# A hybrid attention encoder on one core: values turned on VectorE in 32 by 32 blocks instead of on TensorE, and stored in 128-byte pieces

## The chip, the cores and the metric

The kernel runs on one core of a Trainium2 chip. A core has five engines with instruction streams of their own: PE (TensorE, the matrix engine, which also turns tiles by a matmul with the identity), DVE (VectorE), ACT (ScalarE), POOL (GpSimd) and SP (SyncE, which here issues nearly all DMAs, in one queue). On-chip memory is SBUF, 128 partitions wide; matmuls write to PSUM banks, of which there are eight; everything else lies in DRAM. The metric is the device time of one execution in microseconds (us), lower is better. Before the change it is 1909.06 us (median of 3 runs, 1908.71 to 1910.85).

## The reference, cut to what matters

One encoder layer is applied to two groups of tokens (2048 and 512) with shared weights. A combined projection makes ten pieces; branch A is neighbourhood attention on a grid 64 tokens wide, branch B windowed attention with two key/value heads.

```python
u = rms_norm(h, norm_g)
proj = u @ w_in
qa, ka, va, za, qb, kb, vb, zb, ga, gb = jnp.split(proj, cuts, axis=-1)
o_a = neighbourhood_attention(qa, ka, va, na_rpb, n)      # softmax(q k^T / 8 + bias) @ v
o_b = window_attention(qb, kb, vb, t5_bias, sink, n)
y_a = (o_a * jax.nn.silu(za)) @ w_proj_a
y_b = (o_b * jax.nn.silu(zb)) @ w_proj_b
merged = jax.nn.sigmoid(ga) * y_a + jax.nn.sigmoid(gb) * y_b
return h + merged @ w_out                                 # then a final rms_norm
```

All values are 32-bit floats. The projection leaves features on the partitions and tokens along the free axis. The product of probabilities and values needs the values the other way, with tokens (keys) on the partitions: somewhere `va` and `vb` have to be turned. That turning is what the change is about.

## The kernel before

**Precision by splitting.** Each operand x of a matmul is held as a high part h (x cast to the matmul's reduced type) and a low part l = x - h, and a product is made of three matmuls, h·h, h·l and l·h. So each tensor that is written for a later matmul is written twice, h beside l.

**Windows and features.** The 2560 tokens are handled as five windows (here also called token blocks) of 512 tokens (`WTOK`), numbered 0 to 4. The projection's outputs are 42 features of 128 columns: QA is 0 to 3, KA 4 to 7, VA 8 to 11, ZA 12 to 15, QB 16 to 19, KB 20, VB 21, ZB 22 to 25, then the gates. A VA feature holds two heads of 64 columns.

**Stages.** (1) `beside` projects features of window 4 while the operands for windows 0 and 1 are prepared. (2) A pass over all 42 features in 21 pairs, with the windows 0 and 1 (`pairs`, called by `pass_`). (3) `beside` again, and a second pass with windows 2 and 3. (4) Attention of all windows, with the dense layers mixed in. (5) The end of window 4. Stages 2 and 3 are the passes of this document; by the trace the first runs from about 130 us, the second from about 650 us, and the attention begins near 985 us.

**A pair in a pass.** Two features by two windows are a 2 by 2 block product, done with Strassen's seven products (`product`, line 762) in place of eight. Each product is 12 matmuls of 128x128 by 128x512. Sums of weights for it are made on POOL (`sides`, lines 728 to 741) and split by ACT and DVE (`split_part`, lines 189 and 190); weights are fetched two pairs ahead (`wraw`, `raw`). The product results lie in five PSUM banks (`pa`, `pc`, `pe`, ...). Four of them per pair become finished features: `store` adds what is missing, and hands the result on by kind. The order of the pairs is the list `order`, taken two by two: QA, QA, KA, KA, VA, VA, QB, QB, KB with VB, ZA, ...

**A value feature before.** `store` adds into a tile `tkv`; for VA `columns` (line 263 is its work in `combine`) writes it with the tokens permuted, so that 128 neighbouring columns are 16 grid columns by 8 rows. Two products later (`later(lag[0], ...)`, counted off by `tick`, which `product` calls) `put_v` turns it: `transposed` (line 606) does four 128x128 matmuls against the identity into a PSUM bank `vt`; ACT copies the high part (line 235) and DVE subtracts for the low part (line 236) into `vn`; SP stores `vn` to DRAM (`va` for branch A, two DMAs; `vb` for branch B, one).

**Tiles that matter.** `vn`, `evq`, `evk` and `eva`, that is all finished features on their way to DRAM, rotate through the four buffers of tag `ev` in the pool `ev`: a fifth has to wait until the store of the first has landed. `tkv` rotates through three buffers of tag `t`.

**What sets the order.** In stages 1 to 3 the orders of PE and of SP are those of the program text (`manual_schedule`), the orders of DVE, ACT and POOL are set by a scheduler that plays a time model. SP issues its DMAs in order and waits at the head for what the next one needs. The DMAs on SP's queue carry eight completion semaphores in turn, and each issue waits for the DMA that had the same semaphore before, that is for the one eight places earlier.

**The readers of the values.** In the attention of branch A `unit_a` loads `va` and picks, for block b of 8 grid columns, the slice `v_block(b)` of its middle axis (line 1037): the store puts the even blocks in places 0 to 3 and the odd ones in places 4 to 7.

Of the kernel before, what the change touches and what calls it, by code (L numbers as in the profile page):

```python
# [10 lines left out]
F32R = mybir.dt.float32r  # L11
# [6 lines left out]
P = 128  # L18
# [33 lines left out]
def a_kind_width(kind):  # L52
# [17 lines left out]


def v_block(b):

    return b % 2 * 4 + b // 2


def b_blocks(w, n):
# [10 lines left out]
def encoder_block(ctx: ExitStack, tc: tile.TileContext, xT, x_end, w_in, w_pa, w_pb, w_o, norm_g, final_g,  # L88
# [41 lines left out]
    def move(out, in_):  # L130
        last_move[0] = nc.sync.dma_start(*(f32(a) if a.dtype == F32R else a for a in (out, in_)))
        return last_move[0]
# [418 lines left out]
    def later(steps, fn, *args):  # L551
        queue.append([steps, fn, args])
# [49 lines left out]
    def transposed(dst, src, nch, n):  # L602
# [5 lines left out]
        dv = dst[:n, :, :nch].rearrange("p g c (h f) -> p c g h f", h=2)  # L608
        split(dv[:, :, :, 0, :], dv[:, :, :, 1, :], tv)

    def put_v(br, w, p, t):
        vn = ev.tile([P, 2, 4, P], F32R, tag="ev", name="vn")
        transposed(vn, t, 4, P)
        if br == "a":

            for x in range(2):
                dst = va_d[p][:, w * 64 : (w + 1) * 64, 4 * x : 4 * x + 4].rearrange("g p k f -> p g k f")
                move(dst, vn[64 * x : 64 * x + 64])
        else:
            move(vb_d[w * WTOK : (w + 1) * WTOK].rearrange("(c p) g f -> p g c f", p=P), vn)  # L620

    def put_v_meta(br, p, src):
        vm = st.tile([N_META, 2, 1, P], F32R, tag="vm", name="vm", bufs=1)
        transposed(vm, src, 1, N_META)
        if br == "a":
            if p == 0:
                zr = ev.tile([P, WTOK], F32, tag="t", name="zr", bufs=3)[:, :P]
                nc.vector.memset(zr, 0.0)
                for d in vrow_d:
                    move(d.rearrange("c b g f -> (c b g) f"), zr)  # L630
            n = len(META_COLS)
            for y in range(2):
                b = v_block(META_COLS[0] // 8 + y)
                move(vrow_d[p][:, b : b + n].rearrange("c b g f -> c b (g f)"),
                     vm[8 * y : 8 * y + 8].rearrange("m g o f -> m o (g f)").broadcast_to([8, n, 2 * P]))
        else:
            move(vbm_d, vm[:, :, 0])

    def columns(f, t, ps, other, c0, n):

        if VA <= f < ZA:
            r0, r1 = c0 // GRID_W, (c0 + n) // GRID_W
            ps, o = (x.rearrange("p (r b c) -> p b r c", b=8, c=8) for x in (ps, ps if other is None else other[1]))
            other = other and (other[0], o)
            dst = t.rearrange("p (b r c) -> p b r c", b=8, c=8)[:, :, r0:r1]
        else:
            dst = t[:, c0 : c0 + n]
        combine(dst, ps, other)

    def put_kv(f, w, src):  # L650
        if f < VA:
            put_k("a", w, f - KA, src)
        elif f < ZA:
            later(lag[0], put_v, "a", w, f - VA, src)
        elif f == KB:
            put_k("b", w, 0, src)
        else:
            later(lag[0], put_v, "b", w, 0, src)

    def store(f, w, ps, other):  # L660

        if f < KA:
            put_q("a", w, f, ps, other)
        elif KA <= f < ZA or f in (KB, VB):
            src = ps
            if other is not None or VA <= f < ZA or f == VB:
                src = ev.tile([P, WTOK], F32, tag="t", name="tkv", bufs=3)
                columns(f, src, ps, other, 0, WTOK)
            put_kv(f, w, src)
        elif f < QB:  # L670
            put_act(z_d["a", w, f - ZA], AF.Silu, ps, other)
        elif f < KB:
            put_q("b", w, f - QB, ps, other)
        elif f < GA:
            put_act(z_d["b", w, f - ZB], AF.Silu, ps, other)
        else:
            put_gate(w, f, ps, other)
# [202 lines left out]
                pass  # L880
        return a, first, raw1

    order = [*range(0, ZA), *range(QB, ZB), *range(ZA, QB), *range(ZB, 42)]
    both = list(zip(order[::2], order[1::2]))
    firsts = [*range(QA, KA), *range(QB, KB), *range(KA, ZA), KB, VB]
    rest = [f for f in range(GA) if f not in firsts]
# [93 lines left out]
    def unit_a(w, p, h, g, sh):  # L980

        grows, i0, k0, kr = a_window(w)
        R = kr + 1
        kind = a_kind(w)
        t0 = (0 if w == 0 else DEC_SEQ) + k0 * GRID_W
        nt = kr * GRID_W
        c0, C = CG[g]
        n = R * C
        nb, kb = C // 8, R * 8
        hs = slice(64 * h, 64 * h + 64)  # L990
        qs = slice(g * P, (g + 1) * P)
        if g == 0 and h == 0:
            q = sh["q"] = ld.tile([P, 2, 2, WTOK], F32R, tag="q", name="q")
            move(q.rearrange("p h i t -> p h (i t)"), qa_d[w, p].rearrange("(h d) j x -> (d j) h x", h=2))
        if g == 0 and h == 1:
            z = sh["z"] = ld.tile([P, WTOK], F32, tag="z", name="z")
            move(z, z_d["a", w, p])
        if g == 0:
            kd = sh["kd"] = ld.tile([P, R, GRID_W], F32R, tag="kd", name="kd")
            move(kd[:, 1:, :].rearrange("p r c -> p (r c)"),  # L1000
                 ka_d[p][hs].rearrange("d i t -> (d i) t")[:, t0 : t0 + nt])
            move(kd[:, 0, :], kam_d[p][hs].rearrange("d i t -> (d i) t"))
            v = sh["v"] = ld.tile([P, 8, P], F32R, tag="v", name="v", bufs=3)
            move(v[8:kb], va_d[p][h, t0 // 8 : t0 // 8 + kb - 8])
            move(v[:8], vrow_d[p][:, :, h])
            b = sh["b"] = ld.tile([P, a_kind_width(2)], F32, tag="ba", name="ba")
            move(b[:, : a_kind_width(kind)], bias_a[kind][2 * p + h])
        q, kd, v, z, bias = (sh.get(x) for x in ("q", "kd", "v", "z", "b"))
        yield
        if g == 0 and h == 0:  # L1010
            sh["y"] = at.tile([P, WTOK], F32, tag="y32", name="y32")
        y32 = sh["y"]
        s = ps_s.tile([P, WTOK], F32, tag="s", name="s")
        sv = s[:, :n].rearrange("p (r c) -> p r c", r=R)
        nc.tensor.matmul(sv, q[:, h, 0, qs], kd[:, :, c0 : c0 + C], start=True, stop=False)
        nc.tensor.matmul(sv, q[:, h, 1, qs], kd[:, :, c0 : c0 + C], start=False, stop=True)
        b0 = R * (0, 24, 24, 56)[g]
        nm = scores_max(s, n, bias[:, b0 : b0 + n])
        pr = at.tile([P, 2 * HALF], F32, tag="pr", name="pr", bufs=3)[:, :WTOK]
        sm = sums_of()[:, :1]  # L1020
        exps(pr[:, :n].rearrange("p (b r c) -> p r b c", b=nb, c=8), sv.rearrange("p r (b c) -> p r b c", c=8), nm, sm)
        yield
        normalise(pr[:, :n], inverse(sm), on_act=g == 1)
        yield
        tp = ps_p.tile([P, WTOK], F32, tag="tp", name="tp")
        for i, b in enumerate(A_ORDER[g]):
            nc.tensor.transpose(tp[:kb, i * P : (i + 1) * P], pr[:, b * kb : (b + 1) * kb], ident)  # L1027
        a = slice(A_FIRST[g], A_FIRST[g] + 2 * nb - 1, 2)
        tb = tp[:kb, : nb * P].rearrange("p (b t) -> p b t", t=P)
        nc.scalar.copy(ph_[:kb, a], tb)  # L1030
        nc.vector.tensor_sub(pl_[:kb, a], tb, f32(ph_[:kb, a]))  # L1031
        yield
        if g == 1:
            sh["o"] = ps_o.tile([P, WTOK], F32, tag="o", name="oa")
        o = sh.get("o")
        for i, (part, b, x, gs) in enumerate(A_PRODUCTS[g]):
            vb = v[:kb, v_block(b), :]
            cols = slice(gs[0] * P, (gs[-1] + 1) * P)
            src = (ph_ if part == "h" else pl_)[:kb, x : x + len(gs)].rearrange("p b t -> p (b t)")

            if part == "h":
                nc.tensor.matmul(o[:, cols], vb, src, start=g == 1 and i == 0, stop=False, skip_group_check=True)  # L1042
            else:
                nc.tensor.matmul(o[:64, cols], vb[:, :64], src, start=False, stop=(g, i) == (3, 5),  # L1044
                                 skip_group_check=True)
        if g == 3:
            ol = at.tile([64, WTOK], F32, tag="ol", name="ol", bufs=1)
            nc.scalar.copy(ol, o[64:128])
            nat = "p (g r c) -> p g r c"
            nc.vector.tensor_add(y32[hs].rearrange("p (r g c) -> p g r c", g=4, c=16),  # L1050
                                 o[:64].rearrange(nat, g=4, c=16), ol.rearrange(nat, g=4, c=16))
            if h == 1:
                nc.gpsimd.tensor_mul(y32, y32, z)
                y_split("a", w, p, y32)
        yield
# [509 lines left out]
```

## Time and profile before

| | |
|---|---|
| runs | 1908.71, 1909.06, 1910.85 us |
| profiled execution, its own time | 1908.84 us |
| its span in the trace | 1906.5 us |
| PE busy | 1878.5 us, 99% |
| DVE / ACT / POOL busy | 69% / 60% / 38% |
| share of the 16 DMA engines' time, SP's queue | 66.8% |

A span is shorter than the time of its execution, here by 2.3 us. A row of a group of instructions gives the engine, the operation, the tiles (written <- read), how many there were, and their duration (least, median, largest, or busy time and mean). A waiting instruction shows in the lists of waits, with the one that ended the wait behind the arrow. PE's records overlap, since a matmul begins while the one before is still draining: starts, not durations, tell how long PE is taken.

### The profile page before, as it was taken

The page shows a single profiled execution, that of the slowest core. Times are in us where ns is not written, and L with a number is a line of the kernel's source. Part 1 is how long each engine was busy: PE and PEld are TensorE (multiplying, and loading weights), DVE is VectorE, ACT ScalarE, POOL GpSimd, SP SyncE. Part 2 cuts the span into 40 slices and gives each one's busy share as a digit, 9 for nine tenths or more (in the row PEclk, how much of TensorE's full clock was granted, in tenths as well). Part 3 has the DMA queues.
Part 4 walks back from the last instruction along what each step waited for, and adds up shares of the span by engine and source line. Part 5 has one row for each costly group of instructions (what it writes and reads, how often), then busy time and mean ns, then how long its engine had stood idle before and what let it go on. Part 6 is the DMA issues. An engine that isn't in the chain of part 4 may idle for free.

```text
span 1906.5 us, 29720 instructions
## 1 busy us (share of the span) xinstructions
PE 1878.5 (99%) x9925; PEld 1599.4 (84%) x9925; DVE 1320.3 (69%) x2887; ACT 1147.6 (60%) x2515; POOL 731.9 (38%) x556
## 2 busy tenths in 40 slices
PE   8999999999999999999999999999999999999998
PEld 6998888888888888888878888888888888888886
DVE  8886455556477544445457788878987887888874
ACT  6454443434464444444356787797788788878932
POOL 2005342323103232323223335655844773585420
PEclk9999999999999999999999999999999999999999
DMA  7667554645296765644368877977986996697473
GB/s 261 218 190 293 175 198 165 218 174 177 83 353 218 239 210 194 194 138 160 105 207 289 254 217 261 294 223 242 319 270 185 307 316 217 197 326 252 124 289 141
DMA packets 223760, 423.78 MB, mean 222 GB/s; under 512 B 49640, under 2 KB 90808, under 8 KB 222072
## 3 DMA queue, kind: packets, MB, share of 16 engines
q1 hardware_dynamic: 223320, 421.88, 66.8%
q8 instruction: 79, 1.29, 0.3%
q14 instruction: 73, 0.60, 0.1%
q10 hardware_dynamic: 288, 0.01, 0.0%
HBM read 303.07 MB, written 118.74 MB: 221 GB/s over the span
## 4 chain that ended last, share of the span: by engine, by line
PE 75%; DVE 9%; ACT 6%; DMA 5%; issue 3%; POOL 2%; SPq 0%; ACTq 0%; DVEq 0%; POOLq 0%
PE pa L762 21%; PE pe L762 10%; PE pc L762 5%; PE mm L135 4%; PE mm L137 4%; PE mm L136 4%; PE tp L1027 2%; PE pso L137 2%; PE pso L135 2%; PE pso L136 2%; PE tp L1129 1%; PE oa L1044 1%; PE oa L1042 1%; DVE s L953 1%; DMA wo<-wos 1%
## 5 line engine op out<-in xcount | busy, mean ns | idle before, releaser
L190 POOL TENSOR_TENSOR wt<-wraw,wt 128x512 fp32r<-128x512 f32 x164 | 215.4, 1331 | 288.2 <-ACT wt L189 288.1
L762 PE MATMUL pa<-u,wt 128*128 128x512 f32 x1008 | 242.9, 390 | 0.0
L762 PE MATMUL pa<-u,x 128*128 128x512 f32 x984 | 237.8, 390 | 0.0
L189 ACT CAST wt<-wraw 128x512 fp32r<-128x512 f32 x312 | 177.9, 620 | 73.8 <-PE mm L137 37.6
L762 PEld LDWEIGHTS pa<-u,wt 128*128 128x128 f32 x1008 | 188.7, 188 | 39.0
L762 PEld LDWEIGHTS pa<-u,x 128*128 128x128 f32 x984 | 183.9, 188 | 38.1
L733 POOL TENSOR_TENSOR s<-wraw,raw 128x512 f32<-128x512 f32 x40 | 57.9, 1447 | 271.7 <-DVE x L190 271.7
L135 PE MATMUL mm<-u,wt 128*128 128x512 f32 (+2 forms) x416 | 151.6, 364 | 7.3 <-ACT u L316 7.3
L728 POOL TENSOR_TENSOR s<-raw 128x512 f32<-128x512 f32 x40 | 60.0, 1500 | 253.3 <-DMA raw<-in_w_in_dram 137.0
L136 PE MATMUL mm<-u,wt 128*128 128x512 f32 (+2 forms) x416 | 147.5, 355 | 1.5 <-DVE u L317 1.5
L137 PE MATMUL mm<-u,wt 128*128 128x512 f32 (+2 forms) x416 | 147.5, 355 | 0.8 <-DVE wt L190 0.8
L190 DVE TENSOR_TENSOR wt<-wraw,wt 128x512 fp32r<-128x512 f32 x148 | 104.6, 746 | 61.6 <-ACT wt L189 61.5
L762 PE MATMUL pe<-u,wt 128*128 128x512 f32 x504 | 121.9, 391 | 0.0
L762 PE MATMUL pc<-u,wt 128*128 128x512 f32 x504 | 121.1, 389 | 0.0
L1031 DVE TENSOR_TENSOR pl<-tp,ph 128x512 fp32r<-128x512 f32 (+7 forms) x160 | 98.8, 617 | 24.0 <-ACT ph L1030 22.3
L762 PE MATMUL pe<-u,x 128*128 128x512 f32 x480 | 115.3, 389 | 0.0
L960 ACT ACTIVATE pr<-s,nm 128x384 f32<-128x384 f32 (+5 forms) x160 | 91.3, 571 | 37.9 <-DVE nm L953 35.4
L762 PEld LDWEIGHTS pc<-u,wt 128*128 128x128 f32 x504 | 94.6, 188 | 19.6
L762 PEld LDWEIGHTS pe<-u,wt 128*128 128x128 f32 x504 | 94.2, 188 | 19.4
L741 POOL TENSOR_TENSOR s<-wraw,s 128x512 f32<-128x512 f32 x40 | 52.9, 1322 | 146.2 <-DVE wt L190 146.2
L1030 ACT CAST ph<-tp 128x512 fp32r<-128x512 f32 (+7 forms) x160 | 84.7, 529 | 38.7 <-PE tp L1027 36.5
L135 PE MATMUL pso<-mh,wt 128*128 128x512 f32 x256 | 107.1, 418 | 0.0
(238 smaller groups left out, 5050.7 us busy)
## 6 DMA issues: line engine op xcount, KB each, us to landing
wraw<-in_w_in_dram SPq DMA_DIRECT2D x86, 512.0 KB
qa<-evq SPq DMA_DIRECT2D x20, 1024.0 KB
raw<-in_w_in_dram SPq DMA_DIRECT2D x40, 512.0 KB
q<-qa SPq DMA_DIRECT2D x20, 1024.0 KB
wraw<-in_w_o_dram SPq DMA_DIRECT2D x32, 512.0 KB
kbt<-kb SPq DMA_DIRECT2D x32, 384.0 KB
qb<-evq SPq DMA_DIRECT2D x20, 512.0 KB
ka<-evk SPq DMA_DIRECT2D x20, 512.0 KB
```

The lines of the kernel that those rows point to most:

```text
L135: nc.tensor.matmul(ps, wh, uh, start=first, stop=False)
L136: nc.tensor.matmul(ps, wh, ul, start=False, stop=False)
L137: nc.tensor.matmul(ps, wl, uh, start=False, stop=last)
L189: nc.scalar.copy(h, r)
L190: low[0] = (eng or lo_eng[0]).tensor_sub(l, r, f32(h)).ins
L728: eng.tensor_add(s1, a21, a22)
L733: eng.tensor_sub(s3, a11, a21)
L741: eng.tensor_sub(s4, a12, s2)
L762: nc.tensor.matmul(ps, wt[:, a, s], u[:, b, kk, :], start=first and kk == 0 and i == 0, stop=kk == 3 and i == 2, skip_group_check=True)
L960: nc.scalar.activation(out, s, AF.Exp, bias=nm, scale=-1.0, accum_out=sm)
L1030: nc.scalar.copy(ph_[:kb, a], tb)
L1031: nc.vector.tensor_sub(pl_[:kb, a], tb, f32(ph_[:kb, a]))
```

## The change

For the windows 0 to 3 the four matmuls against the identity go, and with them the permuted write. `put_v_blocks` takes `tkv` as soon as it is made: DVE turns it in blocks of 32 by 32 (`nc.vector.transpose`; two instructions of 256 tokens for VA, whose read pattern gathers 4 grid rows by 8 grid columns as the 32 tokens of a block; one of 512 tokens for VB), ACT copies the high part, DVE subtracts for the low part, all in one `ev` tile named `evv`. One product later `store_v_blocks` issues eight DMAs. A block of 32 features by 32 tokens gives pieces of 32 floats, 128 bytes; four quarters of the features, each in a high and a low part, belong to one token, and each DMA puts 512 such pieces side by side in the token's row. Window 4 still goes through `put_v`; since blocks now lie in their natural order in `va` (`v_block` is gone), its store for VA has steps of two, and is four DMAs in place of two. The order of the pairs becomes QA, QA, VA, KA, KA, VA, QB, ...: the two VA pairs are three places apart.

```diff
-def v_block(b):
-    return b % 2 * 4 + b // 2
...
+    def put_v_blocks(br, w, p, t):
+        e = ev.tile([P, 2, WTOK], F32R, tag="ev", name="evv").rearrange("p i t -> p (i t)")
+        ev4 = e.rearrange("p (b i f) -> p b i f", i=2, f=32)
+        h, l = ev4[:, :, 0], ev4[:, :, 1]
+        for x in range(2) if br == "a" else ():
+            c = slice(x * 256, (x + 1) * 256)
+            nc.vector.transpose(f32(l[:, 8 * x : 8 * x + 8]), t[:, c].rearrange("p (r b c) -> p b r c", r=4, c=8))
+        if br == "b":
+            nc.vector.transpose(f32(l), t)
+        nc.scalar.copy(h, f32(l))
+        nc.vector.tensor_sub(l, f32(l), f32(h))
+        later(1, store_v_blocks, br, w, p, e)
+
+    def store_v_blocks(br, w, p, e):
+        for q in range(4):
+            rows, g, f0 = slice(32 * q, 32 * q + 32), q // 2, q % 2 * 32
+            for x in range(2):
+                if br == "a":
+                    t0 = w * 64 + 32 * x
+                    dst = va_d[p][g, t0 : t0 + 32].rearrange("t b (i f) -> t (b i) f", i=2)[:, :, f0 : f0 + 32]
+                    src = e[rows, x * WTOK : (x + 1) * WTOK].rearrange("p (b f) -> p b f", f=32)
+                else:
+                    c0 = 64 * x + f0
+                    dst = vb_d[w * WTOK : (w + 1) * WTOK, g, c0 : c0 + 32].rearrange("(b t) f -> t b f", t=32)
+                    src = e[rows].rearrange("p (b i f) -> p b i f", i=2, f=32)[:, :, x]
+                move(dst, src)
...
             for x in range(2):
-                dst = va_d[p][:, w * 64 : (w + 1) * 64, 4 * x : 4 * x + 4].rearrange("g p k f -> p g k f")
-                move(dst, vn[64 * x : 64 * x + 64])
+                for g in range(2):
+                    move(va_d[p][g, w * 64 : (w + 1) * 64, x::2], vn[64 * x : 64 * x + 64, g])
...
+    def put_values(br, w, p, src):
+        if w < NWIN - 1:
+            put_v_blocks(br, w, p, src)
+        else:
+            later(lag[0], put_v, br, w, p, src)
...
-                columns(f, src, ps, other, 0, WTOK)
+                combine(src, ps, other)
...
-    order = [*range(0, ZA), *range(QB, ZB), *range(ZA, QB), *range(ZB, 42)]
+    order = [*range(0, KA), VA, VA + 1, *range(KA, VA), VA + 2, VA + 3, *range(QB, ZB), *range(ZA, QB), *range(ZB, 42)]
...
-            vb = v[:kb, v_block(b), :]
+            vb = v[:kb, b, :]
```

The order in which instructions stand shows what moves. On SP, in the first pass around the first VA pair (VA 8 and 9 are `va_107` and `va_108`), before the change (`wraw` and `raw` are weights, `xa` tokens for the second pass, `ka` and `qb` stores of other features; an "x2" counts equal rows in sequence):

```order
L131 DMA ka_100<-evk 256x1x512 x2
L131 DMA va_107<-vn 64x2x512 x2
L131 DMA ka_99<-evk 256x1x512
L131 DMA wraw<-in_w_in_dram 128x1024
L131 DMA raw_2284<-in_w_in_dram 128x1024
L131 DMA xa<-in_xT_dram 128x2x512
L131 DMA va_108<-vn 64x2x512 x2
L131 DMA va_109<-vn 64x2x512 x2
L131 DMA wraw<-in_w_in_dram 128x1024
L131 DMA raw_2439<-in_w_in_dram 128x1024
L131 DMA xa<-in_xT_dram 128x2x512
L131 DMA va_108<-vn 64x2x512 x2
```

And with the change, on the same engine, around the same pair:

```order
L126 DMA qa_64<-evq 256x1x1024
L126 DMA va_107<-evv 512x1x32 x8
L126 DMA qa_60<-evq 256x1x1024
L126 DMA qa_63<-evq 256x1x1024
L126 DMA wraw<-in_w_in_dram 128x1024
L126 DMA raw_1997<-in_w_in_dram 128x1024
L126 DMA xa<-in_xT_dram 128x2x512
L126 DMA va_108<-evv 512x1x32 x8
L126 DMA ka_97<-evk 256x1x512
L126 DMA va_108<-evv 512x1x32 x8
L126 DMA wraw<-in_w_in_dram 128x1024
L126 DMA raw_2167<-in_w_in_dram 128x1024
```

A feature's store is eight issues in place of two, and at most sixteen of them stand between two fetches of weights. On PE, in the second pass, before:

```order
L762 MATMUL pc<-u_4883,wt 128x512 x12
L606 MATMUL vt<-ident,tkv 128x128 x4
L762 MATMUL pa<-u_5252,x_5789 128x512 x12
L762 MATMUL pe<-u_5261,x_5789 128x512 x12
L606 MATMUL vt<-ident,tkv 128x128 x4
L762 MATMUL pa<-u_4884,wt 128x512 x12
```

And with the change, at a place of the same pass:

```order
L793 MATMUL pc<-u_4921,wt 128x512 x12
L793 MATMUL pa<-u_5290,x_5865 128x512 x12
L793 MATMUL pe<-u_5299,x_5865 128x512 x12
L793 MATMUL pa<-u_4922,wt 128x512 x12
```

The rows of line 606 are gone from the passes: PE has 20 rows of four such matmuls less (5619 rows for 5639), and beside these its order is the same to the end. On DVE, at the first VA pair, with the change:

```order
L258 TENSOR_TENSOR tkv<-pc,s_2098 128x512
L234 SCALAR_TENSOR_TENSOR evk<-tkv,evk 128x512
L615 STREAM_TRANSPOSE evv<-tkv 128x8x32 x2
L619 TENSOR_TENSOR evv<-evv 128x16x32
L258 TENSOR_TENSOR tkv<-pe,u_2012 128x512
L185 TENSOR_TENSOR x_2045<-raw_1840,x_2045 128x512
```

A value feature has two transposes (one for VB) and a subtraction here, where it had the subtraction alone (`vn<-vt,vn`, line 236). After the passes the orders of all engines are the same as before.

More of the change, by code (lines that the diff above doesn't have):

```diff
@@ L632, in put_v_meta @@
             for y in range(2):
-                b = v_block(META_COLS[0] // 8 + y)
-                move(vrow_d[p][:, b : b + n].rearrange("c b g f -> c b (g f)"),
+                b = META_COLS[0] // 8 + y
+                move(vrow_d[p][:, b : b + 2 * n - 1 : 2].rearrange("c b g f -> c b (g f)"),
                      vm[8 * y : 8 * y + 8].rearrange("m g o f -> m o (g f)").broadcast_to([8, n, 2 * P]))
@@ L653, in put_kv @@
         elif f < ZA:
-            later(lag[0], put_v, "a", w, f - VA, src)
+            put_values("a", w, f - VA, src)
         elif f == KB:
@@ L657, in put_kv @@
         else:
-            later(lag[0], put_v, "b", w, 0, src)
+            put_values("b", w, 0, src)
     def store(f, w, ps, other):
```

## The prediction

> **What bounds the kernel now.** I read the page's first part, then PE's own timeline in the passes, then the lists of waits.
>
> ```profile
> span 1906.5 us, 29720 instructions
> PE 1878.5 (99%) x9925; PEld 1599.4 (84%) x9925; DVE 1320.3 (69%) x2887; ACT 1147.6 (60%) x2515; POOL 731.9 (38%) x556
> ```
>
> PE is busy for 99% of the span. PE's records overlap, so this alone does not say that PE sets the pace. The windows and the timeline do. The columns of the first fence are the stretch and its length, then each engine's busy us, the granted PE clock, and the DMA engines' share; the second has start, length, and the matmuls in a row.
>
> ```profile
> 135.00:330.00 195.00, 195.00 (x899) 161.90 (x898) 109.34 (x160) 87.18 (x152) 78.90 (x56) 1.00 0.63 213
> 655.00:775.00 120.00, 119.90 (x549) 98.89 (x548) 59.01 (x89) 51.56 (x93) 34.55 (x26) 1.00 0.64 205
> ```
>
> ```profile
> 202.45 2.88 PE L762 MATMUL pa<-u,x 128*128 128x512 f32 x12
> 205.17 2.89 PE L762 MATMUL pe<-u,x 128*128 128x512 f32 x12
> 207.90 0.60 PE L606 MATMUL vt<-ident,tkv 128*128 128x128 f32 x4
> 208.25 3.01 PE L762 MATMUL pa<-u,wt 128*128 128x512 f32 x12
> 211.10 2.88 PE L762 MATMUL pe<-u,wt 128*128 128x512 f32 x12
> ...
> 225.19 2.88 PE L762 MATMUL pe<-u,x 128*128 128x512 f32 x12
> 227.91 0.60 PE L606 MATMUL vt<-ident,tkv 128*128 128x128 f32 x4
> ...
> 231.12 0.60 PE L606 MATMUL vt<-ident,tkv 128*128 128x128 f32 x4
> ...
> 234.32 0.60 PE L606 MATMUL vt<-ident,tkv 128*128 128x128 f32 x4
> ...
> 237.53 2.88 PE L762 MATMUL pa<-u,wt 128*128 128x512 f32 x12
> ```
>
> In both passes (135 to 330 and 655 to 775 hold their value features) PE has no idle time at a full clock, and a product starts 2.72 us after the one before (205.17 - 202.45) wherever nothing stands between them. ACT, in turn, waits for PE to read the weight tiles out, so the operands are ready and PE is late:
>
> ```profile
> ACT x L189 <- PE pe L762: 15.4, 8, 2.2
> ACT wt L189 <- PE pe L762: 7.2, 7, 1.1
> ```
>
> (waits of 135 to 330: us in all, times, longest). What PE no longer does in a pass therefore comes off the end, as long as the others keep up.
>
> **The change part by part.** *What PE loses.* From the product at 205.17 to the one at 211.10 are two products and one turn: 5.93 us, less 2 x 2.72 = 5.44, leaves 0.49. From 225.19 to 237.53 are four products and three turns: 12.34 - 10.88 = 1.46, or 0.487 a turn.
>
> ```profile
> L606 PE MATMUL vt<-ident,tkv x100: 270/272/329, 100.0 to 762.8; 128*128 128x128 f32 x100
> L235 ACT CAST vn<-vt x25: 567/579/589, 101.2 to 764.2; 128x512 fp32r<-128x512 f32 x25
> L236 DVE TENSOR_TENSOR vn<-vt,vn x25: 679/684/692, 102.1 to 765.0; 128x512 fp32r<-128x512 f32 x25
> ```
>
> The 100 matmuls are 25 turns, five of each window; window 4 keeps its five. 20 x 0.487 = **9.7 us** off PE's path.
>
> *What DVE and ACT get.* No DVE transpose is in this trace. The nearest row in size takes 0.42 us for 128x256; the dearest DVE group among the finished features has a mean of 1.10 us, for 512 columns:
>
> ```profile
> L263 DVE TENSOR_TENSOR tkv<-mm,rs x20: 402/422/425, 69.8 to 125.9; 128x256 f32<-128x256 f32 x20
> L239 DVE SCALAR_TENSOR_TENSOR evk<-tkv,evk 128x512 fp32r<-128x512 f32 x8 | 8.8, 1100 | 7.8 <-ACT evk L238 7.8
> L190 DVE TENSOR_TENSOR x<-s,x 128x512 fp32r<-128x512 f32 x84 | 62.2, 740 | 45.4 <-ACT x L189 45.4
> L189 ACT CAST x<-s 128x512 fp32r<-128x512 f32 x84 | 52.1, 621 | 58.6 <-PE pa L762 57.5 <-POOL s L733 1.1
> ```
>
> I take 0.42, since that row has the size, 0.34 (half of the 0.68 of the 512 columns of `vn` above) as the lower end and 1.1 as the upper. A feature then has 0.84 us of transposes (0.7 to 2.2). The subtraction and the copy read SBUF in place of PSUM: 0.74 for 0.68, 0.62 for 0.58. DVE gains 0.84 + 0.06 = 0.9 us a feature, 18 us in all; ten features in the window 135 to 330 bring DVE from 109 to 118 of 195 us, and to 132 at the upper end. Idle time hides all of it; if DVE were the pace, it would cost the 18 us.
>
> *What SP and the DMAs get.* An issue of such a store takes 0.6 us, whatever the pieces:
>
> ```profile
> L131 SPq DMA_DIRECT2D va<-vn x40: 574/598/1622, 102.8 to 710.5; - x40
> 305.37 0.60 SPq L131 DMA_DIRECT2D vb<-vn  x1
> SPq L131 <- DVE evq L236: 48.4, 13, 7.9
> SPq L131 <- DVE evk L239: 42.3, 8, 8.6
> SPq L131 <- DVE vn L236: 40.4, 7, 12.9
> ```
>
> Eight are 4.8 us in place of 1.2 (0.6 for VB). For ten features that is 8 x 3.6 + 2 x 4.2 = 37 us more of SP in 135 to 330, where SP stood for 131 us (the last three rows) with nothing to issue. Behind these issues stand other features' stores and the next fetch of weights; the rivals price that. Window 4 has two issues more for each of four features: 4.8 us over some 25 us of a stage in which weights are fetched three features ahead; I put it at nothing, at most its own 4.8.
>
> A piece of 128 bytes does not occur in this trace. Two stores to DRAM frame it: `kbm` has 512 pieces of 72 bytes and `vb` has 1024 of 512 bytes.
>
> ```profile
> 126.94 2.18 SPq L131 DMA_DIRECT2D kbm<-km  x2
> DMA packets 498, 0.05 MB, mean 82 GB/s; under 512 B 490, under 2 KB 490, under 8 KB 498
> q1 hardware_dynamic: 498, 0.05, 79.5%
> ...
> DMA packets 987, 0.51 MB, mean 281 GB/s; under 512 B 0, under 2 KB 987, under 8 KB 987
> q1 hardware_dynamic: 987, 0.51, 105.0%
> ```
>
> The first answer is for 129.7 to 130.3: 0.6 us x 16 engines x 0.795 / 498 = 15 ns of one engine a piece. The second, 306.6 to 308.4: 1.8 x 16 x 1.05 / 987 = 31 ns. By size 128 bytes is nearer the first: 17 ns (15 to 31). A feature's 4096 pieces are then 4096 x 17 / 16 = 4.4 us (3.9 to 7.9) of all engines, less than SP's 4.8 for issuing them. So the store lasts 4.8 us, plus the way to DRAM. For that I use `vb`: issued at 305.37, its pieces, and those of one more store, are through in slice 27 of 40 of 305.4 to 311, at 309.2.
>
> ```profile
> DMA  0000000019999999999999999960000000000000
> ```
>
> That is 3.8 us. An `ev` tile is held for 0.84 + 0.62 + 0.74, up to 2.72 for the one product that the store is put off, 4.8 and 3.8: **13.5 us**. A pair of seven products lasts 19.04 us and has four finished features for four tiles, so each may be held for 19.04. Features can be ready 2.72 us apart; then the second store waits 4.8 - 2.7 = 2.1 us for the first: 15.6. It still fits, with 3.4 to spare. What hides the stores is this slack; when it is gone, ACT or DVE stops at the next tile, PSUM is not emptied, and PE stops.
>
> [...]
>
> **The sum.** The profiled execution took 1908.84 us for its span of 1906.5. 1908.84 - 9.7 = 1899.1; the median of the runs lies 0.2 above it: **1899.3 us**, 0.5% faster. With nothing on other engines late and 0.487 good to 0.05, it is 1898 to 1901.
>
> **The rivals.** *The `ev` tiles run out (the slower side).* Let a store last s. Of two stores in succession the second tile is held 0.84 + 0.62 + 0.74 + 2.72 + 3.8 - 2.72 + 2s = 6.0 + 2s. That passes 19.04 from s = 6.5 us, 25 ns a piece; what is over comes once for each of the four VA pairs of the two passes. At 27 ns (s = 6.9) it is 0.8 x 4 = 3 us: 1902. At 31 ns (s = 7.9), 2.8 x 4 = 11: 1910, no change. [...] For it: the pieces are four to sixteen times as many. Against it: 15 ns for 72 bytes, at DRAM. It decides from 30 ns.
>
> *Weights come late behind the stores on SP (no change).* Between two fetches up to 17 issues now stand, where six and one stood. The start of the first row is when the six began, of the second when the next weights were issued; below are POOL's first sums on such weights and ACT's split of a later one.
>
> ```profile
> 235.23 10.99 SPq L131 DMA_DIRECT2D va<-vn  x6
> 247.04 1.36 SPq L131 DMA_DIRECT2D wraw<-in_w_in_dram  x1
> 240.55 1.29 POOL L729 TENSOR_TENSOR s<-s,wraw 128x512 f32<-128x512 f32 x1
> 252.36 1.14 ACT L189 CAST wt<-wraw 128x512 fp32r<-128x512 f32 x2
> ```
>
> 17 x 0.6 = 10.2 us is no more than the 11.0 that passed before. POOL was done at 241.8, and the splits for the next pair start at 252.4: 10.5 us of cover. So an issue would have to take (11.0 + 10.5) / 17 = 1.26 us before PE sees it; at 1.4 it is 2.3 us at four places, 9 in all: 1908. Single issues did take up to 1.62, but the median is 0.6.
>
> *The turns were hidden.* If PE took up their 0.49 us waiting for something else, nothing would be gained. The rows of ACT waiting for PE speak against it, and no wait of PE is on the list of 135 to 985. That the matmuls don't go is excluded by PE's order.
>
> **Chances and range.** The forecast 0.75; `ev` at 25 to 29 ns (1900 to 1905) 0.06; `ev` at 29 to 32 ns, late weights or hidden turns (within 0.2%, 3.8 us, about the least that a measurement of this kernel tells from none) 0.10; `ev` above that 0.09. Faster 0.81, same 0.10, slower 0.09. The range from 1897 (window 4 and waits at single turns going better than counted) to 1905 holds the first two, 0.81.
>
> **What would show it.** Right: product starts 2.72 us apart throughout the passes, `vt` with 20 matmuls in place of 100, the attention's first loads 9.7 us earlier, later stages as long as before. The transpose's row should read 0.3 to 1.1 us, an issue 0.6, the DMA answer over a store 15 to 20 ns a piece. Wrong: ACT or DVE waiting for "DMA va<-evv", gaps of PE in the pairs after a VA pair, or POOL waiting longer for `raw`. A loss elsewhere, in the attention, would mean that reading `va` in its new order costs something, for which nothing in the loads, as long as before, speaks.

## The result: 0.5% slower

The changed kernel takes 1919.6 us (median of 6 runs, 1916.37 to 1921.52), the kernel before 1909.9. Of the six runs behind the 1909.9 one took 3149.1 us and is left out of the ratio; the other five lie between 1908.44 and 1910.85. The ratio is 1.0048, with a 95% interval of 1.0038 to 1.0058. The forecast was 1899.3, range 1897 to 1905: wrong in sign, by 20 us. The profiled execution took 1919.48 us, with a span of 1917.4.

### The profile page after: what moved, and what is told of

The parts are those of the page before. It is cut to its first block, busy times and chain, and to the rows that moved or that the text cites. A ratio compares the mean times of both kernels' runs of the same rounds, so it can differ in the third digit from the quotient of the medians.

```text
span 1917.4 us, 29825 instructions
## 1 busy us (share of the span) xinstructions
PE 1876.0 (98%) x9845; PEld 1594.3 (83%) x9845; DVE 1343.7 (70%) x2923; ACT 1145.3 (60%) x2515; POOL 731.5 (38%) x556
## 4 chain that ended last, share of the span: by engine, by line
PE 70%; DVE 10%; DMA 9%; ACT 5%; issue 3%; POOL 3%; SPq 1%; DVEq 0%; ACTq 0%; POOLq 0%
PE pa L793 19%; PE pe L793 9%; PE pc L793 5%; PE mm L132 3%; PE mm L130 3%; PE mm L131 3%; PE pso L132 2%; PE pso L130 2%; PE pso L131 2%; PE tp L1058 2%; DMA wo<-wos 2%; PE tp L1160 1%; SPq L126 1%; DMA sgb<-gb 1%; DVE wt L185 1%
## 5 line engine op out<-in xcount | busy, mean ns | idle before, releaser
L793 PE MATMUL pa<-u,x 128*128 128x512 f32 x984 | 242.1, 396 | 11.5 <-ACT u L804 11.5
L185 DVE TENSOR_TENSOR wt<-wraw,wt 128x512 fp32r<-128x512 f32 x148 | 110.2, 782 | 53.2 <-ACT wt L184 53.0
L793 PEld LDWEIGHTS pe<-u,x 128*128 128x128 f32 x480 | 90.1, 188 | 18.7
```

The costliest lines, as they stand in the source:

```text
L185: low[0] = (eng or lo_eng[0]).tensor_sub(l, r, f32(h)).ins
L793: nc.tensor.matmul(ps, wt[:, a, s], u[:, b, kk, :], start=first and kk == 0 and i == 0, stop=kk == 3 and i == 2, skip_group_check=True)
```

## The profile after

The first part of the page and the windows of the changed kernel (columns as in the prediction; the middle one lies between the two value stretches; the second pass begins in it, near 578 us and not near 650 as put above, and its first VA pair too):

```profile
span 1917.4 us, 29825 instructions
PE 1876.0 (98%) x9845; PEld 1594.3 (83%) x9845; DVE 1343.7 (70%) x2923; ACT 1145.3 (60%) x2515; POOL 731.5 (38%) x556
```

```profile
135.00:330.00 195.00, 193.04 (x869) 159.69 (x868) 124.16 (x181) 88.79 (x156) 79.68 (x56) 1.00 0.70 214
330.00:655.00 325.00, 320.19 (x1400) 264.04 (x1399) 196.88 (x293) 149.53 (x266) 74.28 (x54) 0.99 0.58 202
655.00:775.00 120.00, 115.28 (x497) 94.87 (x496) 65.91 (x97) 51.00 (x92) 32.20 (x23) 0.97 0.71 197
```

80 matmuls are gone (9925 to 9845), as they should be. But PE, which had no idle time in the passes, is short of 2.0, 4.8 and 4.7 us in the three stretches, and the mean granted clock falls to 0.99 and 0.97 in the last two. The list of PE's waits from 135 to 985, empty before, now has one entry (us in all, times, longest):

```profile
PE pa L793 <- ACT u L804: 11.5, 5, 4.7
```

`product` is line 793 now, `u` the copy of a block product out of PSUM by ACT that frees `pa` for the next one. PE's timeline at the two largest of the five waits:

```profile
642.10 2.88 PE L793 MATMUL pe<-u,wt 128*128 128x512 f32 x12
649.45 5.49 PE L793 MATMUL pa<-u,x 128*128 128x512 f32 x12 [4.47 <-ACT u L804]
654.74 2.97 PE L793 MATMUL pa<-u,wt 128*128 128x512 f32 x12
...
706.50 2.88 PE L793 MATMUL pe<-u,wt 128*128 128x512 f32 x12
714.10 5.49 PE L793 MATMUL pa<-u,x 128*128 128x512 f32 x12 [4.72 <-ACT u L804]
719.39 0.78 PE L793 MATMUL pa<-u,wt 128*128 128x512 f32 x2
```

After each, the next product takes 5.29 us from start to start (654.74 - 649.45) in place of 2.72, at half the clock. The windows around the first (the granted clock is the third number from the end):

```profile
640.00:644.50 4.50, 4.50 (x21) 3.72 (x21) 0.87 (x2) 1.11 (x2) 1.69 (x2) 1.00 0.60 121
649.40:654.80 5.40, 5.35 (x13) 4.20 (x14) 3.73 (x5) 2.07 (x4) 2.05 (x2) 0.50 0.73 126
```

So the passes lose 11.5 us of waiting and 2 x (5.29 - 2.72) = 5.1 us of slow clock. Less the predicted 9.7 that is 6.9 us; measured up to the first matmul behind the second pass, it is 991.56 - 983.25 = 8.3. Counted from start to start the difference goes: the five products begin 12.3 us late in all, they and the two behind the slow ones take 5.8 us more than 2.72 each, and 12.3 + 5.8 - 9.7 = 8.4. The two rows, of before and of after:

```profile
983.25 0.39 PE L135 MATMUL mm<-u,wt 128*128 128x512 f32 x1
```

```profile
991.56 0.39 PE L130 MATMUL mm<-u,wt 128*128 128x512 f32 x1
```

**What ACT was doing.** ACT works in order, and beside the projection it does *side work*: `prep_end` splits the output weights for later stages in the second pass (tile `wos`), `prep_ahead` squares and sums the tokens of the coming windows in the first (tile `xa`). Both load with a DMA on SP. ACT's timeline after, up to the copy that PE waits for at 649.45:

```profile
642.97 0.62 ACT L184 CAST wos<-wos 128x512 fp32r<-128x512 f32 x1 [7.43 <-DMA wos<-in_w_o_dram]
643.50 0.58 ACT L256 COPY tkv<-pa 128x512 f32<-128x512 f32 x1
645.03 0.62 ACT L618 CAST evv<-evv 128x512 fp32r<-128x512 f32 x1 [0.95 <-DVE evv L615]
...
648.29 0.62 ACT L618 CAST evv<-evv 128x512 fp32r<-128x512 f32 x1 [1.60 <-DVE evv L615]
648.81 0.58 ACT L804 COPY u<-pa 128x512 f32<-128x512 f32 x1
```

and the same place before, with PE's two products beside it:

```profile
641.55 0.62 ACT L189 CAST wos<-wos 128x512 fp32r<-128x512 f32 x1 [8.14 <-DMA wos<-in_w_o_dram]
...
645.32 0.57 ACT L773 COPY u<-pa 128x512 f32<-128x512 f32 x1
```

```profile
643.51 2.88 PE L762 MATMUL pe<-u,wt 128*128 128x512 f32 x12
646.23 2.88 PE L762 MATMUL pa<-u,x 128*128 128x512 f32 x12
```

This is the main reading. Before, ACT stood 8.1 us for the side load as well, and its copy ended at 645.32 + 0.57 = 645.89, only 0.34 us before PE began the next product. The place was on the edge, and no list of waits shows an edge. Now three things add up. The load is used 1.42 us later (642.97 - 641.55). The work behind it, up to the copy, takes 5.84 us in place of 3.77: the results of a VA pair are finished here, where before those of a KA pair were, and the two high parts of the values wait for the transposes (0.95 and 1.60; before, this stretch had one wait of 0.56). And PE comes 1.41 us earlier (its product is due at 642.10 + 2.72 = 644.82, before at 646.23). 1.42 + 2.07 + 1.41 - 0.34 = 4.6 us; the product starts 649.45 - 644.82 = 4.63 late.

The transposes are late for the same load. DVE's timeline of the changed kernel:

```profile
643.63 0.69 DVE L185 TENSOR_TENSOR wos<-wos 128x512 fp32r<-128x512 f32 x1 [7.36 <-ACT wos L184]
644.24 0.76 DVE L615 STREAM_TRANSPOSE evv<-tkv 128x256 f32<-128x256 f32 x2
```

DVE stands 7.36 us for its own half of the split and turns the values only then. On SP the load itself is held up:

```profile
622.13 5.30 SPq L126 DMA_DIRECT2D va<-evv  x8
...
631.51 1.24 SPq L126 DMA_DIRECT2D wo<-wos  x1
640.03 0.38 SPq L126 DMA_DIRECT2D wos<-in_w_o_dram  x1
```

and before:

```profile
628.78 1.21 SPq L131 DMA_DIRECT2D wo<-wos  x1
```

`wos` has one buffer, so its next load may go only when the store of the last result (`wo`) has landed: SP stands from 632.75 to 640.03, and everything queued behind it too. That store is itself issued 2.7 us later than before, behind eight value stores that take SP for 5.3 us.

**The second place**, at 709, is the same point of a pair: the pair of QB features behind the second VA pair, in both kernels. ACT after, then before, and PE's product before:

```profile
705.60 0.62 ACT L184 CAST wos<-wos 128x512 fp32r<-128x512 f32 x1 [8.01 <-DMA wos<-in_w_o_dram]
...
713.47 0.58 ACT L804 COPY u<-pa 128x512 f32<-128x512 f32 x1
```

```profile
698.11 0.62 ACT L189 CAST wos<-wos 128x512 fp32r<-128x512 f32 x1 [4.82 <-DMA wos<-in_w_o_dram]
...
704.12 0.59 ACT L773 COPY u<-pa 128x512 f32<-128x512 f32 x1 [1.64 <-PE pa L762]
```

```profile
707.42 3.01 PE L762 MATMUL pa<-u,x 128*128 128x512 f32 x12
```

Here the late load is the larger part. It is used 7.49 us later, while PE's product is due only 1.80 later (706.50 + 2.72 = 709.22): 5.69 us against PE. From the load to the copy it is 7.87 us in place of 6.01, of which 1.64 were a wait for PE: 3.50 more. The slack was 707.42 - 704.71 = 2.71, and those 1.64. 5.69 + 3.50 - 2.71 - 1.64 = 4.84 us; the product starts 714.10 - 709.22 = 4.88 late.

In the first pass the same happens at 194 and, by 0.5 us, at 253 with `xa`, a token load that is issued behind the value stores (at 178.57 for the first, with eight value stores from 169.12 on ahead of it). The fifth wait, 0.3 us at 410, is in a pair of gates with no value feature near. ACT's waits for side loads and transposes, 135 to 985, before and after:

```profile
ACT wos L189 <- DMA wos<-in_w_o_dram: 58.9, 15, 8.1
ACT xa L458 <- DMA xa<-in_xT_dram: 16.0, 7, 3.9
```

```profile
ACT wos L184 <- DMA wos<-in_w_o_dram: 66.8, 15, 8.0
ACT xa L453 <- DMA xa<-in_xT_dram: 33.7, 7, 7.1
ACT evv L618 <- DVE evv L615: 13.9, 10, 2.2
```

**The prices that were forecast** are in the groups of the tile `evv` (ns: least, median, largest), and in the DMA answer for 248 to 252:

```profile
L615 DVE STREAM_TRANSPOSE evv<-tkv x32: 398/418/447, 165.5 to 712.5; 128x256 f32<-128x256 f32 x32
L126 SPq DMA_DIRECT2D va<-evv x128: 549/627/2427, 169.1 to 725.2; - x128
```

```profile
q1 hardware_dynamic: 3152, 0.39, 66.2%
```

0.42 us for a transpose (0.42 forecast), 0.63 for an issue (0.6), and 4 us x 16 x 0.662 / 3152 = 13.4 ns for a piece of 128 bytes (17, range 15 to 31, so a little under the range).

## The experiments

The theory (theory 1 below): the loss is ACT standing for side loads, with the value steps between them and the copy that PE needs. Rivals: the long run of store issues on SP, the size of the pieces, the new order of the pairs, and too few `ev` tiles. Runs 1 to 4 are compared with a median of 1909.6 for the kernel before, runs 5 to 8 with one of 1909.8.

### 1. Side work of the second pass kept away from the value pairs

```
-    ... prep_end(), [... for j in range(2 * KT) for i in (1, 0, 2)]
+    ... prep_end(), [... for j in (0, 3, *range(6, 20)) for i in (1, 0, 2)]
```

The list says after which products a step of `prep_end` runs; nothing is left out, it only comes elsewhere.

> The changed kernel with one list different: in the second pass the steps that split the output weights (load `wos`, split it on ACT and DVE, store it as `wo`) skip the pairs next to the two VA pairs and run in later pairs instead. The V stores and the DVE transposes stay as they are. Theory 1 (ACT stands at a late load of side work, `wos` or `xa`, that waits in SP's queue, and the value features behind it then make ACT's next copy late): PE's two waits at 644.6 and 709.0 of 4.9 and 5.1 us go, and with them the two products after them that took 5.3 instead of 2.7 us: 15 us less than the changed kernel, about 1904. Theory 2 (the 128-byte pieces or their number of issues hold the `ev` tiles): the V stores are the same, so 1917 to 1921. Theory 3 (the turn itself, ACT waiting for DVE and DVE for ACT): the same, 1917 to 1921.

Measured: 1902.89, ratio 0.9969 (0.9957 to 0.9982). PE's list of waits on ACT shrinks to

```profile
PE pa L793 <- ACT u L804: 2.3, 3, 1.6
```

and what is left are waits of the first pass, 1.6 us at 194 and under 0.5 each at 252 and 409, which the edit doesn't touch. The stores, their issues and their pieces are all still there. Moving the side work by some products is worth 16.7 us (1919.6 - 1902.9) and turns the loss into a gain.

### 2. The same store in two DMAs with long rows

```
 def store_v_blocks(br, w, p, e):
-    for q in range(4): ... for x in range(2): move(dst, src)    # 8 DMAs of 512 pieces, 128 B
+    for x in range(2): move(va_d[p][x, w*64:(w+1)*64].rearrange("t (h b) f -> (t h) (b f)", h=2), e[:, x*WTOK:(x+1)*WTOK])
```

VB becomes one DMA. The values lie in another order in DRAM than the attention reads.

> The changed kernel with the store of a value feature written by two DMAs of whole rows (2 KB pieces; one DMA of 4 KB pieces for VB) in place of eight of 128-byte pieces. The turn on DVE stays. The values then lie in DRAM in another order than the attention wants, so the output is not the reference's; bytes and all other work are the same. Theory 1: SP is 3.6 us a feature earlier with the fetches and the side loads behind it, so the waits of PE shrink to the part that the turn adds: 1903 to 1910. Theory 2: all of the loss goes, 1899 to 1901. Theory 3: the loss stays, 1915 to 1921.

Measured: 1903.93, ratio 0.9968 (0.9956 to 0.9979). ACT waits 11.7 us for `xa` (33.7) and 48.7 for `wos` (66.8). One wait of PE is left in the passes:

```profile
643.94 4.61 PE L787 MATMUL pa<-u,x 128*128 128x512 f32 x12 [3.35 <-ACT u L798]
648.39 2.92 PE L787 MATMUL pa<-u,wt 128*128 128x512 f32 x12
```

So the stores do make the side loads later, and without their length four of the five waits go. At 709 the stretch from the load to the copy is as long as in the change (692.96 to 700.83, 7.87 us), and PE does not wait, since the load comes early enough. The wait at 640 stays. There the load still has to wait for a store of `wo` to land, and is used 640.42 - 636.87 = 3.55 us before PE's product is due, where before it was 646.23 - 641.55 = 4.68. The stretch to the copy is 6.44 us (to 643.31) in place of 3.77. 1.13 + 2.67 - 0.34 = 3.46, and the product starts 643.94 - 640.42 = 3.52 late: the longer stretch alone is more than the slack. That the stores alone are not the cause follows from runs 1 and 2 together: each edit by itself takes away most of the loss, so it takes both, a late side load and a place where it stands ahead of the copy.

### 3. Eight DMAs of long rows

```
+    dst = va_d[p][g, t0 : t0 + 32, 4 * h : 4 * h + 4].rearrange("t b f -> t (b f)")   # 32 rows of 2 KB
+    move(dst, e[rows, x * WTOK : (x + 1) * WTOK])
```

As many issues as in the change, but 32 pieces each.

> The changed kernel with eight DMAs a value feature as it has, but each of 32 pieces of 2 KB in place of 512 pieces of 128 bytes (values in another order in DRAM, so the output is not the reference's). Number of issues and bytes are the same, only the size of the pieces differs. If the pieces' size is the cost (theory 2, pieces): 1899 to 1903. If the number of issues on SP is (theory 2, issues, and theory 1): 1915 to 1921, with the same waits of PE. Theory 3: 1915 to 1921.

Measured: 1905.98, ratio 0.9981 (0.9972 to 0.9991), between the two expectations. It doesn't separate issues from pieces as it was meant to, since an issue of 32 rows takes a median of 0.42 us, not 0.63: the run of issues became shorter too. Two waits are left, at 640 and 703:

```profile
PE pa L791 <- ACT u L802: 3.3, 2, 2.8
```

Whether SP's time or the DMA engines' makes more of the delay stays open.

### 4. Value pairs late in the pass

```
-    order = [*range(0, KA), VA, VA + 1, *range(KA, VA), VA + 2, VA + 3, ...]
+    order = [*range(0, VA), *range(QB, ZB), *range(ZA, QB), *range(ZB, 40), *range(VA, ZA), 40, 41]
```

There is no side work left there, so the pairs can't meet it; but two VA pairs follow each other, the hardest case for the `ev` tiles and for SP.

> The changed kernel with another order of the pairs: the two VA pairs are the 19th and 20th of each pass, where no side work (tokens for the second pass, output weights) is left; stores, pieces, issues and turns are the same. Theory 1: no late side load stands before the value features on ACT, so PE's waits in the VA pairs go in both passes: 1899 to 1902, the forecast. Theory 2: two VA pairs in sequence make sixty-four issues in 38 us, so the loss stays or grows, 1917 to 1930. Theory 3: the loss stays, 1915 to 1921.

Measured: 1922.7, ratio 1.0067 (1.0052 to 1.0082): theory 1's number missed by over 20 us. The time lies in theory 2's range, but the waits are not where theory 2 has them: in the pairs PE's list has a single wait on ACT of 0.2 us, even where SP issues 56 value stores, with one other between them, from 490 to 529, and where ACT waits 4.9 us in all for such stores to land. The loss is at the ends of both passes, where the following stage begins:

```profile
525.90 2.88 PE L793 MATMUL pa<-u,x 128*128 128x512 f32 x12
535.07 0.80 PE L130 MATMUL mm<-u,wt 128*128 128x512 f32 x1 [6.29 <-ACT u L311]
...
978.88 2.88 PE L793 MATMUL pa<-u,x 128*128 128x512 f32 x12
990.77 0.79 PE L130 MATMUL mm<-u,wt 128*128 128x512 f32 x1 [9.02 <-ACT u L311]
```

PE stops for 535.07 - 525.90 - 2.72 = 6.5 us and for 9.2 us, each followed by matmuls that start 0.43 us apart (537.30 - 536.88 and 993.20 - 992.77) in place of 0.23 (2.72 / 12). On SP the load of the next stage's weights stands behind the stores:

```profile
517.35 11.46 SPq L126 DMA_DIRECT2D va<-evv  x16
528.92 0.55 SPq L126 DMA_DIRECT2D wraw<-in_w_in_dram  x1
```

ACT waits 14.1 us for it. This is the prediction's rival "Weights come late behind the stores on SP", at a place that the change itself doesn't have. For the theory the run says two things: in the pairs PE has nothing to wait for once no side load stands there; and theory 1 was too narrow, since any load will do that is queued behind the stores and has no cover.

### 5. Side work kept away in both passes

Run 1's edit, and the same for `prep_ahead`:

```
-    steps = [(0, 1), *((n, i) for n in range(1, KT) for i in (0, 1)), (KT, 0), (9, 0), (9, 1),
-             *((j, i) for j in range(10, 18) ...)]
+    steps = [*((j + i, 1 - i) for j in (0, 1, 3, 4, 6, 7, 8, 9) for i in (0, 1)), (11, 0), (11, 1),
+             *((j, i) for j in range(12, 20) ...)]
```

> The kernel of e1_side_work_away, and in the first pass too the side work (tokens `xa` loaded for the second pass, squared on ACT) skips the places just after the stores of the two VA pairs and ends two pairs later. Stores, pieces, turns and the order of the pairs are those of the change. Theory 1 (ACT stands at a late side load): PE's waits at 194 and 253 go as well, 2.7 us and more; no wait of PE on ACT's copy over 1 us is left in either pass, and the time is 1898 to 1901, the forecast of 1899.3. Theories 2 and 3: no better than e1, 1902 to 1904, since e1 was then better by accident of its order.

Measured: 1900.04 (1897.74 to 1903.38), ratio 0.9947 (0.9933 to 0.9961). It beats both kernels. Its windows, and its one row of the first matmul behind the passes:

```profile
135.00:330.00 195.00, 195.00 (x865) 161.44 (x864) 114.55 (x164) 92.14 (x159) 80.61 (x58) 1.00 0.71 217
330.00:655.00 325.00, 325.00 (x1451) 269.44 (x1450) 207.38 (x314) 150.04 (x267) 78.22 (x55) 1.00 0.59 203
655.00:775.00 120.00, 120.00 (x531) 99.41 (x530) 66.05 (x99) 54.19 (x97) 35.20 (x25) 1.00 0.70 200
```

```profile
973.18 0.39 PE L130 MATMUL mm<-u,wt 128*128 128x512 f32 x1
```

PE is full at full clock again, and the passes end 983.25 - 973.18 = 10.1 us earlier than before, where 9.7 had been forecast. Stores, issues and pieces are those of the change. ACT still waits 33.1 us for `wos` and 14.8 for `xa`, but in places where that costs nothing.

### 6. A second landing place for the side load

```
+        t = st.tile([P, 4, WTOK], F32R, tag="x0", name="wos", bufs=1)
         for c in range(2):
             for k in range(KT):
-                t = st.tile(...); raw = f32(t[:, 0])
+                raw = f32(t[:, 3 * (k % 2)])
```

The next `wos` load may go before the last `wo` store has landed; the side work stays where the change has it.

> The changed kernel with one wait less: the output weights of the second pass are loaded by turns into two slots of one tile, so that SP need not stand at the load of `wos` until the store `wo` before it has landed. All pairs, places, stores and turns are as in the change. Theory 1, with SP's stand at that load as the link: the loads are issued 6 to 8 us earlier, ACT is not late in the VA pairs of the second pass, PE's waits at 644.6 and 709.0 go: 1903 to 1906; the first pass keeps its waits. If the load is late for another reason (the DMA engines are full, the turns), the waits stay: 1915 to 1920.

Measured: 1909.94, ratio 0.9999 (0.9988 to 1.001): half of the loss against run 5, and not the 1903 to 1906 expected. ACT still waits 58.4 us for `wos`. PE's waits fall from 11.5 to 6.6 us:

```profile
PE pa L793 <- ACT u L804: 6.6, 4, 2.4
```

SP's stand for the landing is one link of the chain, not the whole of it: at 640 the load is issued at 631.33 in place of 640.03, but used only at 639.83, 8.5 us later, where in the change it is 2.9. What the DMA engines do first in that time (the weights and the `wo` store are ahead, value stores behind) is not separated by any run.

### 7. The old order of the pairs

```
-    order = [*range(0, KA), VA, VA + 1, *range(KA, VA), VA + 2, VA + 3, ...]
+    order = [*range(0, ZA), *range(QB, ZB), *range(ZA, QB), *range(ZB, 42)]
```

> The changed kernel with the order of the pairs of the kernel before: the two VA pairs in sequence as the 5th and 6th of each pass, beside the side work that stands there. Theory 1: the VA pairs meet the side loads there just the same, so PE waits in both passes, 1912 to 1925. If the new order of the pairs is itself what loses: 1899 to 1905. If the `ev` tiles or SP run out when 64 issues come in 38 us: above 1925.

Measured: 1920.88, ratio 1.0054 (1.0039 to 1.007), the change's own time within what can be told. The waits move (those over 0.5 us to 251, 415, 688 and 715) and stay as large:

```profile
PE pa L793 <- ACT u L804: 14.2, 5, 5.1
```

The order isn't the cause; it only picks the places.

### 8. The kernel before, with the side work of run 5

The kernel before with both lists of run 5, as a control.

> The kernel before the change, with the side work of both passes moved to the same places as in e5_both_passes: values are turned on PE and stored in wide pieces. It tells whether moving the side work gains by itself. PE has no waits in the passes before, so by theory 1 nothing is to be had: 1907 to 1911. If it comes out near 1900, the moved side work, and not its meeting with the value features, made e1 faster.

Measured: 1910.02, ratio 0.9999 (0.999 to 1.0008). Where PE has no waits to lose, moving the side work gains nothing: the 9.7 us of run 5 (1909.75 - 1900.04) are the change's own.

## Why the prediction was wrong, step by step

- **What PE loses, 20 turns x 0.487 = 9.7 us: right.** Run 5, with nothing late, is 9.7 us below the kernel before in the medians and 10.1 in the passes, and run 8 shows that none of it comes from the side work.
- **What DVE and ACT get: the prices right, "Idle time hides all of it" wrong. This step failed**, and with it the sum's condition "With nothing on other engines late". A transpose took 0.42 us as forecast; DVE's busy time grew by 23.4 us (1343.7 - 1320.3) in place of 18. The cover was counted as idle time of a window (DVE 109 of 195 us busy), an average. Work of 0.9 us a feature is hidden by idle time only where that stands next to it. At 640 the engines do have idle time, 7.4 us of it, but ahead of the work: they stand, in order, for a side load. Behind it the copy had 0.34 us to spare, and the new chain DVE, ACT, DVE asks for 2.07 more. With the step below, it cost 11.5 us of waiting and 5.1 of slow clock.
- **What SP and the DMAs get: the prices near the forecast (0.63 us an issue, 13.4 ns a piece); what stands behind the stores incomplete. This step failed too.** "Whatever the pieces" does not hold either: run 3's issues of 32 pieces took 0.42 us. The step named "other features' stores and the next fetch of weights" and priced the cover of the weights alone. The side loads were left out, though the list of ACT's waits had both before the change (58.9 and 16.0 us): an engine that already waits for a load has no cover for that load. At 709 the load came 5.7 us later against PE. With short stores (run 2) the kernel is 15.7 us faster than the change.
- **The `ev` tile: right.** The profile lists one wait of ACT for a value store, 1.4 us, and it lies in the stretch ahead of the wait at 709. But `tq`, which that instruction reads, was finished by DVE only 0.08 us before it began (706.87 + 0.68, against 707.63), and in run 6 the same gap of 1.4 us is put down to `tq`: the tile cost PE next to nothing. (A wait of 2.3 us for a store of QA, at 635, lies ahead of the stand for `wos`, which ends last.) Run 4's VA pairs in succession don't stop PE in the pairs either. Rival one falls, at 13.4 ns a piece against the 25 at which it would have begun.
- **Weights come late: right that the change's weights don't, right in the mechanism elsewhere.** Run 4 shows it at 6.5 and 9.2 us, at the start of a stage, where nothing has been fetched ahead.
- **"The turns were hidden": no.** They were on the path, by run 5.
- **The price of the small pieces: a little under the range.** Three stretches of the change's trace that hold such stores (170 to 174, 248 to 252, 625 to 628) give 13.3 to 13.4 ns for 128 bytes, less than the 15 of the row on 72-byte stores and far from the 32 above which 0.09 of the chances lay.
- **What would show it:** the list of what would show it wrong had "gaps of PE in the pairs after a VA pair". They came just there: four of the five stand at the fifth of its own products of the pair that follows a VA pair. But they came by ACT's copy, not by a tile.
- **Reading `va` in its new order costs nothing that shows.** From the first matmul behind the passes to the end of the span it is 923.3 us before (1906.5 - 983.25) and 927.2 in run 8, which reads as before; 925.8 in the change and 922.7 to 928.2 in runs 1 to 7.

What stays open: how the late side loads divide between SP's issues and the DMA engines (run 3 doesn't settle it, nor does run 6); how much of the 4.6 and 4.8 us at the two places each term would cost alone, since the two sums share it out only by argument; and some 1 to 2 us between the passes' 8.3 us and the medians' 9.7, no more than the 3.9 us by which the stages behind the passes differ between the two executions that read as before.

## What to carry to other kernels

Look for edges, not only for waits: at each place where an in-order engine stands for something, take what it does next that the bounding engine needs, and subtract its end from the time at which that is due. An idle share is no cover, and a wait that costs nothing today is the one at which a few added steps, or a faster bounding engine, begin to cost. Where a change takes work off the bounding engine and loses, move the optional work away from the new stores before giving the change up: here two lists of numbers made 1919.6 into 1900.0.

## What the runs showed of the hardware

Some short stops of PE cost more than their length here. In the change, waits of 4.47 and 4.72 us were each followed by 5.29 us for one product of 2.72: 2.57 us on top. The granted clock was 0.50 from 648.03 to 654.85 and from 712.88 to 719.71, 6.8 us each time, and 1.00 before and behind. In run 2 a wait of 3.35 us gave a product of 4.45 (648.39 - 643.94), in run 3 one of 2.82 us a product of 5.29 (649.11 - 643.82). Other waits had no such tail: in the change's first pass the product after 1.50 us took 2.87 (198.98 - 196.11), at a clock of 1.00. Of two waits in run 6 the one of 2.27 us was followed by a product of 2.85 (649.20 - 646.35), the one of 2.43 by one of 4.23 (711.11 - 706.88), with a clock of 0.53 from 706.4 to 710.

All the waits named here with a tail are of 2.43 us or more, those without one of 2.27 or less. What decides whether a wait brings the low clock, no run shows.
